# A channel shuffle on one core: the first two tiles cut into pieces of 4, 6, 10 and 20 KB a partition where they were 4, 8 and 28 KB

## The chip, the core and the metric

The kernel runs on one core of a Trainium2 chip. The metric is device time in microseconds (us), from the start of the program to its end; before the change the median of three runs is 316.1 us (316.05 to 316.12). A profile of one execution stands beside it. In the profile the engines are named PE (TensorE), DVE (VectorE), ACT (ScalarE), POOL (GpSimd) and SP (SyncE). This kernel computes on DVE alone; SP and ACT only issue DMAs.

## The reference

The input is a float32 tensor of 16 x 64 x 64 x 256, 67.11 MB. The 256 channels of every pixel are seen as 8 groups of 32, and the two are swapped, so that channel g*32 + j moves to place j*8 + g. No arithmetic is done: every byte is read once and written once, in another order within its row of 1 KB.

```python
x = x.reshape(batch, h, w, groups, channels_per_group)
x = x.transpose(0, 1, 2, 4, 3)
x = x.reshape(batch, h, w, c)
```

## The kernel before

The 65,536 pixels are taken as a flat list of rows of 256 floats (1 KB). A piece of q KB a partition is 128 x q consecutive rows: partition p holds q of them in one run, so a piece is one contiguous block in HBM, and each partition's share of it is contiguous too.

The list `_SLOTS` (line 12) says how the rows are cut. Each entry is a tile, and a tile is a list of pieces whose sizes are in KB a partition. Before the change there are 15 tiles: the first has pieces of 4 and 8 KB, the second one of 28 KB, then come twelve of 38 KB, and one of 16 KB. All tiles have the size of the biggest, 38 KB a partition; a smaller one uses the front of it.

Three things happen to a piece. SP issues its load into `in_tile` (line 55). DVE copies it to `out_tile`, reading in the transposed order and writing in a straight line (lines 57 to 60). ACT issues its store from `out_tile` (line 61). Within a tile all loads are issued first, and then copy and store go piece by piece.

The order on each engine is that of the program; nothing reorders it. What makes one engine wait for another is the data and the buffers. There are two input buffers (`_IN_BUFS`), used in turn: the load of tile k + 2 waits for the copies of tile k. There are three output buffers (`_OUT_BUFS`): the copies of tile k + 3 wait until the stores of tile k have landed. The loads are in one DMA queue (q1 in the profile, issued by SP), the stores in another (q10, issued by ACT); both are served by the same 16 DMA engines.

Of the kernel before, what the change touches and what calls it, by code (L numbers as in the profile page):

```python
# [1 line left out]

# [4 lines left out]


F32 = mybir.dt.float32
P = 128  # L10

_SLOTS = [[4, 8], [28]] + [[38]] * 12 + [[16]]
_IN_BUFS = 2
_OUT_BUFS = 3


@with_exitstack
def kernel(
    ctx: ExitStack,
    tc: tile.TileContext,  # L20
    x: bass.AP,
    groups: bass.AP,
    out: bass.AP,
):
    nc = tc.nc
    b, h, w, c = x.shape
    G = int(groups)
    CPG = c // G
    assert G * CPG == c
    assert sum(map(sum, _SLOTS)) * P == b * h * w  # L30
    biggest = max(map(sum, _SLOTS))

    x_flat = x.rearrange("b h w c -> (b h w c)")
    out_flat = out.rearrange("b h w c -> (b h w c)")

    in_pool = ctx.enter_context(tc.tile_pool(name="in_pool", bufs=_IN_BUFS))
    out_pool = ctx.enter_context(tc.tile_pool(name="out_pool", bufs=_OUT_BUFS))

    def rows(flat, first, q):

        return flat[first * c : (first + P * q) * c].rearrange("(p f) -> p f", p=P)

    ctx.enter_context(tc.manual_schedule(engines=None))
    first = 0
    for parts in _SLOTS:
        in_tile = in_pool.tile([P, biggest * c], F32, name="in_tile")
        out_tile = out_pool.tile([P, biggest * c], F32, name="out_tile")
        at = 0
        pieces = []
        for q in parts:  # L50
            pieces.append((q, first, slice(at * c, (at + q) * c)))
            first += P * q
            at += q
        for q, start, cols in pieces:
            nc.sync.dma_start(out=in_tile[:, cols], in_=rows(x_flat, start, q))  # L55
        for q, start, cols in pieces:
            nc.vector.tensor_copy(  # L57
                out=out_tile[:, cols].rearrange("p (i j g) -> p i j g", j=CPG, g=G),
                in_=in_tile[:, cols].rearrange("p (i g j) -> p i j g", g=G, j=CPG),
            )  # L60
            nc.scalar.dma_start(
                out=rows(out_flat, start, q), in_=out_tile[:, cols]
            )


# [1 line left out]
_INS = ['x', 'groups']  # L67
_OUTS = [((16, 64, 64, 256), 'float32')]

_NUMBERS = {'groups': 8}  # L70


# [26 lines left out]
```

## Time and profile before

| what | value |
| --- | --- |
| median of three runs | 316.1 us (316.05 to 316.12) |
| span of the profiled execution, first to last instruction | 314.4 us |
| bytes read and written | 67.11 MB and 67.11 MB, 427 GB/s over the span |
| DVE busy | 119.0 us, 16 copies |
| copy of 38 KB, mean of 12 | 8.79 us |
| first copy starts | 4.06 us |
| last copy (16 KB) starts, takes | 294.54 us, 3.87 us |
| first store issued (ACT) | 5.19 us |

The page gives no time of the profiled execution other than its span; 1.7 us lie between the span and the median. A span starts with the first instruction and ends with the last. The 40 slices of a row each cover 7.9 us, and a digit 9 means busy for 90% or more. A DMA share is the busy share of the 16 DMA engines, by packets; in a short stretch it can go over 1, because a packet is counted in the stretch in which it starts. The times from issue to landing of the early transfers:

```profile
in_tile<-in_x_dram SPq DMA_DIRECT2D x1, 3584.0 KB, 14.7
out_dram<-out_tile ACTq DMA_DIRECT2D x1, 3584.0 KB, 30.9
in_tile<-in_x_dram SPq DMA_DIRECT2D x1, 1024.0 KB, 5.4
out_dram<-out_tile ACTq DMA_DIRECT2D x1, 1024.0 KB, 25.0
in_tile<-in_x_dram SPq DMA_DIRECT2D x1, 512.0 KB, 3.3
out_dram<-out_tile ACTq DMA_DIRECT2D x1, 512.0 KB, 14.3
```

A landing counts from the issue, so it contains the time in which the transfer stands behind others.

### The profile page before, as it was taken

How to read it: one execution, taken by the hardware profiler on the slowest of the kernel's cores; microseconds unless marked ns; L12 is line 12 of the kernel's file. 1: busy time of each engine (PE TensorE's matmuls, PEld its weight loads, DVE VectorE, ACT ScalarE, POOL GpSimd, SP SyncE). 2: the span in 40 equal slices, each digit the busy share in tenths (PEclk: the TensorE clock that was granted, in tenths of full speed). 3: DMA queues.
4: the chain of work that ended last, by engine and by line, in shares of the span. 5: the costliest groups of instructions: out<-in, count | busy, mean ns of one | idle time of the engine just before them, and what ended most of it. 6: DMA issues, size and time to landing. Idle time of an engine off the chain costs nothing.

```text
span 314.4 us, 132 instructions
## 1 busy us (share of the span) xinstructions
DVE 119.0 (38%) x16; POOL 0.2 (0%) x4
## 2 busy tenths in 40 slices
DVE  2081907309109109019028028037046055065400
POOL 0000000000000000000000000000000000000000
DMA  7999999999999999999999999999999999999997
GB/s 317 405 441 416 435 416 483 401 465 406 450 421 446 426 436 436 401 470 396 475 396 475 396 470 401 470 401 470 401 450 421 446 426 436 436 417 450 429 421 321
DMA packets 4608, 134.22 MB, mean 427 GB/s; under 512 B 512, under 2 KB 512, under 8 KB 768
## 3 DMA queue, kind: packets, MB, share of 16 engines
q1 hardware_dynamic: 2304, 67.11, 49.8%
q10 hardware_dynamic: 2304, 67.11, 49.4%
HBM read 67.11 MB, written 67.11 MB: 427 GB/s over the span
## 4 chain that ended last, share of the span: by engine, by line
DMA 76%; DVE 19%; issue 0%; SPq 0%; DVEq 0%
DMA in_tile<-in_x_dram 76%; DVE out_tile L57 19%; SPq L55 0%; DVEq L57 0%
## 5 line engine op out<-in xcount | busy, mean ns | idle before, releaser
L57 DVE COPY out_tile<-in_tile 128x9728 f32<-128x9728 f32 (+4 forms) x16 | 119.0, 7440 | 179.4 <-DMA in_tile<-in_x_dram 179.4
L80 POOL MEMSET const-uint8-127<- 128x1 uint8 x1 | 0.1, 103 | 0.0
L80 POOL MEMSET const-bfloat16-1.0<- 128x1 bf16 x1 | 0.1, 102 | 0.0
L80 POOL MEMSET const-float32-1.0<- 128x1 f32 x1 | 0.1, 100 | 0.0
L80 POOL MEMSET const-float32-0.0<- 128x1 f32 x1 | 0.1, 99 | 0.2 <-issue 0.2
## 6 DMA issues: line engine op xcount, KB each, us to landing
in_tile<-in_x_dram SPq DMA_DIRECT2D x12, 4864.0 KB, 37.0
out_dram<-out_tile ACTq DMA_DIRECT2D x12, 4864.0 KB, 42.6
in_tile<-in_x_dram SPq DMA_DIRECT2D x1, 3584.0 KB, 14.7
out_dram<-out_tile ACTq DMA_DIRECT2D x1, 3584.0 KB, 30.9
in_tile<-in_x_dram SPq DMA_DIRECT2D x1, 2048.0 KB, 30.4
out_dram<-out_tile ACTq DMA_DIRECT2D x1, 2048.0 KB, 15.2
in_tile<-in_x_dram SPq DMA_DIRECT2D x1, 1024.0 KB, 5.4
out_dram<-out_tile ACTq DMA_DIRECT2D x1, 1024.0 KB, 25.0
```

The costliest lines, as they stand in the source:

```text
L57: nc.vector.tensor_copy(out=out_tile[:, cols].rearrange("p (i j g) -> p i j g", j=CPG, g=G), in_=in_tile[:, cols].rearrange("p (i g j) -> ...
L80: nc = _bacc.Bacc("TRN2", target_bir_lowering=False, num_devices=1)
```

## The change

Only the list of sizes changes. The first tile now has three pieces, of 4, 6 and 10 KB, and the second tile one of 20 KB; together they are 40 KB a partition as before, so every later tile covers the same rows at the same addresses. There are still 15 tiles, which use the buffers in the same turn. There is one piece more, and so one load, one copy and one store more (17 of each where there were 16). The first 38 KB tile uses the input buffer of the first tile, so its load now waits for three copies rather than two; the second 38 KB tile uses the output buffer of the first tile, so its copy now waits for three stores rather than two.

```diff
-_SLOTS = [[4, 8], [28]] + [[38]] * 12 + [[16]]
+_SLOTS = [[4, 6, 10], [20]] + [[38]] * 12 + [[16]]
 _IN_BUFS = 2
 _OUT_BUFS = 3
```

## The prediction

> **What bounds the kernel now.** I read the page first (busy shares, the slices, the two DMA queues), then busy time by stretch, then the timeline of the first 60 us, then single stretches of the DMA queues to price a packet.
>
> ```profile
> span 314.4 us, 132 instructions
> DVE 119.0 (38%) x16; POOL 0.2 (0%) x4
> DMA  7999999999999999999999999999999999999997
> DMA packets 4608, 134.22 MB, mean 427 GB/s; under 512 B 512, under 2 KB 512, under 8 KB 768
> q1 hardware_dynamic: 2304, 67.11, 49.8%
> q10 hardware_dynamic: 2304, 67.11, 49.4%
> DMA in_tile<-in_x_dram 76%; DVE out_tile L57 19%; SPq L55 0%; DVEq L57 0%
> ```
>
> VectorE (DVE) works 38% of the span. q1 carries the loads, q10 the stores; together their packets occupy the 16 DMA engines for 99.2% of the span, 311.9 of 314.4 us. So the chain of waits, which alternates a load and a copy, is not the limit: each of its loads lasts so long because the engines are full. By stretch (busy DVE, POOL, clock, DMA share, GB/s):
>
> ```profile
> 0.00:1.60 1.60, 0.00 (x0) 0.20 (x4) 1.00 0.00 0
> 1.60:312.00 310.40, 119.04 (x16) 0.00 (x0) 1.00 1.00 432
> 312.00:314.40 2.40, 0.00 (x0) 0.00 (x0) 1.00 0.27 116
> ```
>
> Nothing moves before 1.6 us; then the engines are full until 312.0; the last packets and the final wait take the rest. The whole span is 1.6 us of start, the packets' time, and about 1 us at the end. Only three things can move the end: the packets' own time, an interval in which loads and stores are both missing, and the two ends.
>
> What a packet costs, from stretches with one size (queue: packets, MB, share of 16 engines over the stretch). From 60 to 83 us, both queues with 38 KB a partition:
>
> ```profile
> q1 hardware_dynamic: 144, 4.98, 50.1%
> q10 hardware_dynamic: 144, 4.98, 50.1%
> ```
>
> From 308.6 to 312 us, the 16 KB store alone; then from 3.8 to 5.4 us, the 8 KB load alone; then from 1 to 2 and from 2 to 3 us, the 4 KB load alone:
>
> ```profile
> q10 hardware_dynamic: 94, 1.54, 105.6%
> ...
> q1 hardware_dynamic: 82, 0.67, 101.8%
> ...
> q1 hardware_dynamic: 11, 0.05, 36.9%
> ...
> q1 hardware_dynamic: 71, 0.29, 73.4%
> ```
>
> A load or store leaves 144 packets, 9 per engine: 8 of data, one per partition, and a tiny one (32 tiny ones among the 288 in 23 us). 38 KB: 1.002 x 23 x 16 / 256 = 1.440 us each. 16 KB: 1.056 x 3.4 x 16 / 94 = 0.611. The slope is 0.829 us for 22,528 B, 0.0368 us per 1000 B; the constant is 0.611 - 0.603 = 0.008 us. 8 KB: 1.018 x 1.6 x 16 / 82 = 0.318, a constant of 0.016. The queues take turns packet by packet: 144 against 144 above, and 142 against 141 from 8.5 to 19 us, where stores of 4 KB stand against loads of 28 KB.
>
> **The change part by part.** All edits lie in the first two tiles; bytes, the 12 big tiles and the last one stay.
>
> ```profile
> 4.06 1.09 DVE L57 COPY out_tile<-in_tile 128x1024 f32<-128x1024 f32 x1 [4.06 <-DMA in_tile<-in_x_dram]
> 6.61 2.02 DVE L57 COPY out_tile<-in_tile 128x2048 f32<-128x2048 f32 x1 [1.46 <-DMA in_tile<-in_x_dram]
> 16.36 6.57 DVE L57 COPY out_tile<-in_tile 128x7168 f32<-128x7168 f32 x1 [7.73 <-DMA in_tile<-in_x_dram]
> 30.18 8.82 DVE L57 COPY out_tile<-in_tile 128x9728 f32<-128x9728 f32 x1 [7.25 <-DMA in_tile<-in_x_dram]
> 49.11 8.80 DVE L57 COPY out_tile<-in_tile 128x9728 f32<-128x9728 f32 x1 [10.10 <-DMA in_tile<-in_x_dram]
> ```
>
> 1. One more load and one more store of the same bytes. Per engine 2 x 8 data packets at a constant of 0.008, and 2 tiny ones (no more than 0.01 each): 0.15 us. With the constant of the 8 KB row, 0.28. On the path, since the engines are full. Bounds 0.15 and 0.28; I take 0.2.
>
> 2. Copies. 1.09, 2.02 and 6.57 (9.7 us) become 1.09, about 1.56, 2.48 and 4.77 (9.9; between the rows of 1024, 2048, 4096 and 7168 elements: 1.09, 2.02, 3.87, 6.57). Nothing on the path: DVE stands idle 179 us. SP issues one load more (0.33 us) and ACT one store more (0.36); SP's fourth issue ends near 2.1 us, and the third load keeps the engines until about 8.2.
>
> 3. The first 38 KB load waits for all copies of the first tile. Before, it is issued at 8.7 us with the 28 KB load in the queue until 16.4. After: 1.6 + 0.3 (slow first packets, item 5) + 8 x (0.159 + 0.234 + 0.385) = 8.1, plus 0.9 to landing (the 4 KB load's last packet should end at 1.6 + 0.3 + 1.3 = 3.2; its copy starts at 4.06), so the 10 KB copy starts near 9.1 and ends near 11.7. The cover is the 20 KB load: 8 x 0.761 = 6.1 us and the 4 KB store's packets beside it, so until about 15.6. The new load, issued at 11.7, has first packets some 0.9 later (0.73 to 1.6 for the first one). Were it late, the stores in the queue would still fill the engines. Cost 0.
>
> 4. Out buffers. There are three, so the copy of the second 38 KB tile waits for all stores of the first tile: 16 packets per engine before, 24 after. Before, the 8 KB store lands at 8.65 + 25.0 = 33.6 us and that copy starts at 49.1: 15.5 us spare. After, stores begin near 7 to 9 us (none showed between 5 and 8 us before) and take turns with 8 packets of 20 KB and 16 of 38 KB, the loads up to the second big one. So the 10 KB store's last packet goes out with about the last packet of that load: the spare falls to roughly -2 to +6 us and stays so for the tiles after, both queues moving at one packet each. Where it is negative, DVE shows a wait on a store for the first time. Queued behind it: that store, and the load two tiles on, which SP issues after the copy. That copy ends 9 to 12 us after its load landed, while the next load occupies 23 us; and two stores lie queued. Cost 0; gone only if the copy came another 10 us later.
>
> 5. Slow packets early. In 1 to 2 us the first 4 KB packets took 0.369 x 16 / 11 = 0.54 us each rather than 0.16: 0.26 us, and the first load is unchanged. From 8.5 to 34 us loads beside small stores run over their price:
>
> ```profile
> q1 hardware_dynamic: 142, 4.07, 91.2%
> ...
> q1 hardware_dynamic: 147, 5.10, 81.9%
> ...
> q1 hardware_dynamic: 144, 4.98, 57.6%
> ```
>
> (8.5 to 19, 19 to 34, 34 to 54 us.) 153.2 engine-us against 150.7 by the price, 196.6 against 188.9, 184.3 against 184.5. Divided by 16: 0.16, 0.48, 0. So 0.64 us are lost while 16 small store packets per engine go by, and none later. Part of it is one event: from 31.8 to 33 us, 9 load packets take 0.822 x 1.2 x 16 / 9 = 1.75 us each, not 1.44. If the loss follows the count of small stores (24, or 32 with the 20 KB one), it grows by 0.32 to 0.64; if it was an accident of that execution, it can vanish: -0.64. I take 0, since the largest share sits in one short event.
>
> 6. The end. Stores lag the loads by 8 more packets per engine, so more lies behind the last load: before, it landed at 294.4 with stores until 312. The last copy (3.9 us) and the out buffer it waits for lie under two queued 38 KB stores. From 296 to 306 us stores alone fill 1.01 of the engines, as both queues do. Cost 0.
>
> Two sentences apart: DMA: Bandwidth & Descriptors, section Anatomy of one DMA, gives each DMA a fixed cost of about 2 us (for DMAs issued from GpSimd, an engine that issues none here), which for one more load and one more store would make 316.1 + 4 = 320. The section Rules for kernel authors asks for at least 1 MiB per DMA, which the 4, 6 KB pieces (0.5 and 0.75 MiB) miss; the full stretches above show no such cost where transfers stand queued back to back.
>
> Sum: 0.2 + 0 + 0 + 0 + 0 + 0 = 0.2 us. The profiled span is 314.4, and the median 316.1 is 1.7 above it; the 1.7 is taken as unchanged. 316.1 + 0.2 = 316.3.
>
> **The rivals.**
>
> A, slower: the early loss follows the number of small packets. For it: 0.64 us while small stores ran, 0 after. Against it: the event at 32 us. Price 0.28 + 0.64 = 0.9, so 317.0. It decides from +0.63, that is if each of the 16 more store packets up to the 20 KB one costs about 0.03 us (0.64 / 16 = 0.04).
>
> B, faster: the finer start removes the early loss. At most 0.64 + 0.26 go, less the 0.15: 315.4. Against it: the first load, whose packets are the slowest, is untouched, and stores remain small. Nothing else is to be had: of the span only 2.5 us are outside the packets' time.
>
> C, the buffer wait of item 4 reaches the DMA queues: not only must the load queue run dry (10 us of cover), stores must be gone too, with two of 23 us each in the queue. If one such gap of 3 us came, 319. Nothing speaks for it.
>
> D, the change does nothing: 316.1, inside the forecast.
>
> **How the numbers follow.** A measurement of this kernel tells about 0.2% (0.6 us) from no change: 315.5 to 316.7 counts as the same. Forecast and D 0.80; A 0.12 and C 0.02, slower; B 0.06, faster. Range: from 316.3 down by most of the 0.64 that may vanish, 315.7; up to rival A, 317.0. The likeliest case's own range is 316.1 to 316.6.
>
> **What would show it.** DMA queues: 2448 packets each, not 2304, shares that sum to 99% again, 1.00 between 1.6 and 312. Four small copies at about 1.1, 1.6, 2.5, 4.8 us; the first 38 KB load issued near 11.7, before the 20 KB load is out. From the fourth tile on, DVE idle time that ends with a store, or barely not; the last load landing some us earlier and a longer stretch of stores alone, with the end unmoved. Wrong if any stretch after 2 us has a DMA share clearly under 1, or if 38 KB packets take more than 1.44 us for longer than the first 35 us.

## The result and the profile after

The changed kernel takes 326.36 us (326.24 to 326.42, four runs) against 316.11 us before: a ratio of 1.0321, with a 95% interval of 1.0308 to 1.0334. The prediction was 316.3 us, at most 317.0. The profiled execution's span is 324.6 us, 10.2 more than before.

The page of the changed kernel:

```profile
span 324.6 us, 137 instructions
DVE 120.5 (37%) x17; POOL 0.2 (0%) x4
DMA  8999999999999999999999999999999999999997
q10 hardware_dynamic: 2448, 67.11, 51.0%
q1 hardware_dynamic: 2448, 67.11, 48.3%
```

The packets are those foreseen, 2448 a queue, and the DMA engines are again full nearly all the time: 99.3% of a longer span. So nothing stands still; the same bytes cost more DMA time. q1 (loads) occupies 48.3% of 324.6 = 156.8 us, against 49.8% of 314.4 = 156.6 before. q10 (stores) occupies 165.5 us against 155.3. **All of the 10.2 us are in the stores' packets.**

Busy time by stretch (DVE, POOL, clock, DMA share, GB/s) says when; first the changed kernel, then the one before:

```profile
2.00:60.00 58.00, 27.87 (x6) 0.00 (x0) 1.00 1.02 432
60.00:280.00 220.00, 80.21 (x10) 0.00 (x0) 1.00 1.00 413
```

```profile
2.00:60.00 58.00, 27.30 (x5) 0.00 (x0) 1.00 1.01 427
60.00:280.00 220.00, 80.94 (x10) 0.00 (x0) 1.00 1.00 434
```

The first 60 us, in which all the changed pieces are loaded and nearly all of them stored, are no slower (432 GB/s against 427). From 60 to 280 us, in the 38 KB tiles that the change leaves alone, the full engines move 413 GB/s instead of 434. One period of that stretch in the changed kernel, from the copy at 86.6 to the next at 110.9 us, and the part of it in which DVE does nothing, from 95.7 to 110.8 us:

```profile
q10 hardware_dynamic: 144, 4.98, 52.4%
q1 hardware_dynamic: 144, 4.98, 47.4%
...
q10 hardware_dynamic: 96, 3.11, 52.8%
q1 hardware_dynamic: 96, 3.11, 47.7%
```

A load packet takes 0.474 x 24.3 x 16 / 128 = 1.44 us, as before. A store packet takes 0.524 x 24.3 x 16 / 128 = 1.59 us where it took 1.44, and as long while DVE stands idle (0.528 x 15.1 x 16 / 80 = 1.59), so it isn't the copies that disturb it. Nine 38 KB stores run beside 38 KB loads, 72 packets per engine, and 72 x 0.15 = 10.8 us, of which a few packets at the start are spared.

DVE shows the wait that the prediction's item 4 had as possible:

```profile
DVE out_tile L57 <- DMA out_dram<-out_tile: 159.3, 12, 15.5
DVE out_tile L57 <- DMA in_tile<-in_x_dram: 20.1, 5, 8.6
```

Twelve copies are released by a store and not by a load. It is tempting to call this the cause; the experiments say otherwise.

### The profile page after: what moved, and what is told of

Read it like the earlier page. It is cut to its first block, busy times and chain, and to the rows that moved or that the text cites. A ratio compares the mean times of both kernels' runs of the same rounds, so it can differ in the third digit from the quotient of the medians.

```text
span 324.6 us, 137 instructions
## 1 busy us (share of the span) xinstructions
DVE 120.5 (37%) x17; POOL 0.2 (0%) x4
## 3 DMA queue, kind: packets, MB, share of 16 engines
q10 hardware_dynamic: 2448, 67.11, 51.0%
q1 hardware_dynamic: 2448, 67.11, 48.3%
## 4 chain that ended last, share of the span: by engine, by line
another core or an unknown queue 40%; DVE 29%; DMA 23%; SPq 0%; issue 0%; DVEq 0%
DVE out_tile L57 29%; DMA out_dram<-out_tile 15%; DMA in_tile<-in_x_dram 8%; SPq L55 0%; DVEq L57 0%
## 5 line engine op out<-in xcount | busy, mean ns | idle before, releaser
L57 DVE COPY out_tile<-in_tile 128x9728 f32<-128x9728 f32 (+5 forms) x17 | 120.5, 7090 | 179.5 <-DMA out_dram<-out_tile 159.3
## 6 DMA issues: line engine op xcount, KB each, us to landing
out_dram<-out_tile ACTq DMA_DIRECT2D x12, 4864.0 KB, 63.3
```

Of the source, the lines that this page charges most:

```text
L57: nc.vector.tensor_copy(out=out_tile[:, cols].rearrange("p (i j g) -> p i j g", j=CPG, g=G), in_=in_tile[:, cols].rearrange("p (i g j) -> ...
```

## The experiments

A number made them comparable: the **lag**, how many data packets per DMA engine the stores are behind the loads. The kernel issues the load of tile k + 2 and the store of tile k after the same copy, tile k's. If both landed together, the stores would be exactly 2 tiles, 16 packets, behind. Each turn of one load and one store packet by which the store lands later (2.88 us; 3.03 with slow stores) adds one packet. Both issues, kernel before and then changed kernel (last column: us to landing):

```profile
in_tile<-in_x_dram SPq DMA_DIRECT2D x12, 4864.0 KB, 37.0
out_dram<-out_tile ACTq DMA_DIRECT2D x12, 4864.0 KB, 42.6
```

```profile
in_tile<-in_x_dram SPq DMA_DIRECT2D x12, 4864.0 KB, 39.0
out_dram<-out_tile ACTq DMA_DIRECT2D x12, 4864.0 KB, 63.3
```

Before: 16 + 5.6 / 2.88 = 18. After: 16 + 24.3 / 3.03 = 24, three whole tiles. With 8 data packets per tile and engine, a lag of 16 or 24 means that an engine's load packet and the store packet after it belong to the same one of its 8 partitions, if every whole DMA gives an engine the same partitions in the same order (the trace doesn't name a packet's partition). That became the theory; its rivals were the buffer wait, the small pieces themselves, and the HBM addresses of load and store.

The runs in which every big tile is whole and of 38 KB, in one table. The store packet is the mean of the 38 KB data packets between 100 and 250 us, from the queue's share in that stretch (changed kernel: 0.518 x 150 x 16 / 784 = 1.585; 30.51 MB are 784 packets). Each run but the first two rows is one execution; the kernel before, run on the same chip, took 316.06 to 316.43 beside them.

| run | landing of 38 KB load, store | lag | store packet, us | time, us |
| --- | --- | --- | --- | --- |
| before | 37.0, 42.6 | 18 | 1.44 | 316.1 |
| after | 39.0, 63.3 | 24 | 1.59 | 326.4 |
| e1_hold2 | 39.3, 63.6 | 24 | 1.57 | 327.2 |
| e2_before_hold6 | 36.9, 53.9 | 22 | 1.44 | 316.1 |
| e3_14_16 | 39.5, 39.6 | 16 | 1.59 | 328.5 |
| e4_shift76 | 39.2, 63.5 | 24 | 1.59 | 326.9 |
| f1_lag16_shift76 | 39.2, 39.5 | 16 | 1.58 | 328.3 |
| f2_before_shift | 36.9, 42.5 | 18 | 1.44 | 316.1 |
| f4_8_22 | 34.4, 60.1 | 25 | 1.44 | 319.0 |
| g1_before_hold7 | 39.3, 63.6 | 24 | 1.59 | 328.2 |
| g2_12_18 | 37.4, 48.8 | 20 | 1.44 | 322.2 |
| g4_pad640 | 38.9, 63.1 | 24 | 1.58 | 326.2 |
| h7_after_hold3 | 37.0, 57.0 | 23 | 1.44 | 318.8 |

Every run at 16 or 24 has slow stores, and no other has.

### First runs: hold the first store, change the pieces, shift the addresses

e1 is the changed kernel, with dummy copies on ACT ahead of the first store; e2 is the kernel before with six of them.

```diff
+            if first_store:
+                first_store = False
+                for _ in range(_HOLD):
+                    nc.scalar.copy(out=out_tile[:, 28 * c : 32 * c], in_=in_tile[:, 0 : 4 * c])
             nc.scalar.dma_start(
```

> Same tiles as the changed kernel; ACT makes two dummy copies of 1024 elements (into an unused part of the output buffer) before it issues the first store, which therefore leaves about 1.5 us later. Lag theory (38 KB store packets are slow when stores run exactly 3 tiles, 24 packets per engine, behind the loads, so that the two queues are at the same partition): the lag becomes 3 tiles and about 2 packets, store packets return to 1.44 us, time 316.3 to 317. Theory of the buffer wait (DVE's wait on stores is what costs): stores come later still, the wait grows, 326 or more. Theory of the extra small pieces: they are all there, 326.

327.23 us, and the lag did not move: ACT issued the first store at 5.26 us, while its second dummy copy was still running (the two end at 6.2), and the store landed 11.6 us later, as without a hold (11.8). The edit missed its aim, so the run decides nothing.

> The kernel before with its old pieces (4, 8; 28), but six dummy copies on ACT hold the first store back by some 6.5 us, about six load packets of 28 KB. Lag theory: the lag goes from 2 tiles and 2 packets to 3 tiles and about 0, store packets of 38 KB rise to about 1.58 us and the time to about 326; one packet off and it may stay at 316 to 317. Theory of the small pieces: 316 to 317. Theory of the buffer wait: DVE waits for stores, slower, up to 326.

316.08 us. The first store was issued at 9.48 us rather than 5.19, which made a lag of 22, not 24. Fast, as the lag theory has it for 22, but no test yet.

e3 has other pieces in the changed kernel:

```diff
-_SLOTS = [[4, 6, 10], [20]] + [[38]] * 12 + [[16]]
+_SLOTS = [[4, 6, 14], [16]] + [[38]] * 12 + [[16]]
```

> Pieces 4, 6, 14 and 16 KB: as many transfers as in the changed kernel, but the third load is longer, so stores begin while it runs, some 2 to 3 packets before the second tile's load. Lag theory: lag 2 tiles and 5 to 6 packets, no wait of DVE on stores, 38 KB packets at 1.44 us, 316.3. Theory of the small pieces: 326.

328.54 us, a miss of the lag that was expected. Between 15 and 20 us the stores got ahead, 162 packets against 59 (tiny ones included): the copy of the 14 KB piece, for which the first 38 KB load waits, ends only at 14.8 us. The lag settled at 16 rather than 21 or 22, the other multiple of 8. The run's worth lies in its waits, in which no copy is released by a store:

```profile
DVE out_tile L57 <- DMA in_tile<-in_x_dram: 194.5, 17, 15.7
```

Slow without any wait on the output buffers: **the buffer wait is not the cause.** At a lag of two tiles, ten 38 KB stores run beside 38 KB loads, not nine, and 80 x 0.15 = 12 us fits the 12.5 that this run is over the kernel before.

e4 leaves the order alone and moves the HBM addresses of the 38 KB loads.

```diff
-            nc.sync.dma_start(out=in_tile[:, cols], in_=rows(x_flat, start, q))
+            nc.sync.dma_start(out=in_tile[:, cols], in_=rows(x_flat, start + (_SHIFT if q == 38 else 0), q))
```

> The changed kernel, but each 38 KB load reads x from 76 rows further on (two partitions' worth, 77,824 B), so the output is shifted by 76 rows in these tiles. Order, sizes, buffers and partitions stay; only the HBM addresses that are read while a given store packet runs move, to the relation they had in the kernel before (2 packets apart). If the slow store packets come from load and store being at the same SBUF partition: 326 still. If they come from the HBM addresses of load and store: 316.3.

326.85 us: still slow. But load and store were now three tiles and two packets apart in HBM, not two tiles and two packets as before, so the next runs set this relation itself.

### HBM addresses or partitions

f1 is e3 with a shift of +76 rows, f2 the kernel before with -76; the edit is that of e4.

> Pieces 4, 6, 14 and 16 KB (lag of the stores: 16 packets per engine, slow), but the 38 KB loads read x from 76 rows further on, so the output is shifted there. While a store packet runs, load and store addresses in HBM now stand exactly as in the kernel before (two tiles and two packets apart), but both are at the same SBUF partition. Theory of the same partition (lag a multiple of 8 packets): still slow, 328. Theory of the HBM addresses: 316.3.

328.31 us: with the HBM relation of the kernel before, but at a lag of 16, it is as slow as e3. (The shift can't give the same relation at every packet: at an engine's last ones of a tile, a lag of 18 pairs a store with the load of one tile further on. But were the other store packets at 1.44 us, the mean would be well under the 1.58 that was measured.)

> The kernel before (lag 18 packets, fast), with the 38 KB loads reading x from 76 rows earlier, so the output is shifted there. HBM addresses of load and store now stand two whole tiles apart, as in the slow run with pieces of 4, 6, 14, 16 KB; the partitions stay two packets apart. Same partition: 316.1. HBM addresses: 326 to 328.

316.10 us: with the HBM relation of the slow e3, but at a lag of 18, it is as fast as the kernel before. **The HBM addresses of load and store to one another are not the cause.**

f3 was to take load and store to different partitions at the same lag:

```diff
+                nc.sync.dma_start(out=in_tile[64:, cols], in_=src[64:, :])
+                nc.sync.dma_start(out=in_tile[:64, cols], in_=src[:64, :])
```

> The changed kernel, with each 38 KB load issued as two, partitions 64 to 127 first and then 0 to 63; stores are whole. The packets per engine and the lag of 24 should stay, but load and store are no longer at the same partition at the same time. Same partition: store packets at 1.44 us, 316.5 (12 more tiny packets per engine, 0.1 us). A theory in which the lag itself matters (both queues change transfers at the same moment): 326.

386.98 us, for another reason. From 60 to 100 us:

```profile
q1 hardware_dynamic: 220, 6.69, 65.2%
q10 hardware_dynamic: 222, 5.34, 35.3%
```

The 6.69 MB are 172 load packets, so one takes 0.652 x 40 x 16 / 172 = 2.43 us, and 1.96 from 100 to 250 us (54.0% for 25.76 MB, 662 packets): loads of 64 neighbouring partitions, on all 16 engines, cost far more than whole ones. In the Trainium skill, SBUF — State Buffer, the section "Can I just issue two DMAs to hit both halves?", says that only a transfer over all 128 partitions reaches all 16 ports, and this agrees. Splitting a load adds a tiny packet to each tile's loads alone, too, so the lag did not stay: it fell from 22 at 60 us to 17 at 250 us. The run tells nothing of the theory.

### One packet on either side, and the old pieces at a lag of 24

f4 moves the changed kernel's start by one packet.

```diff
-_SLOTS = [[4, 6, 10], [20]] + [[38]] * 12 + [[16]]
+_SLOTS = [[4, 6, 8], [22]] + [[38]] * 12 + [[16]]
```

> Pieces 4, 6, 8 and 22 KB: as many transfers as in the changed kernel, but the 22 KB load starts some 0.6 us earlier, so one packet more of it should be out before the first store packet: lag 25 rather than 24 (if two: 26). Same partition: store packets at 1.44 us, 316.3, although DVE waits for stores even longer. Theory of the small pieces or of the buffer wait: 326 or more. If a lag of 25 is still slow, neighbouring partitions collide as well.

318.97 us at a lag of 25, store packets back at 1.44 us, although as many pieces are loaded and twelve copies still wait for stores, 152.9 us in all (159.3 in the changed kernel). What is left, 2.5 us over the kernel before beside it (316.43), is not in the stores' price. From 314 us to the end the engines' mean share is 0.04 (16 x 3.2 x 0.04 = 2 engine-us), which is one engine finishing alone:

```profile
314.00:317.20 3.20, 0.00 (x0) 0.00 (x0) 1.00 0.04 15
```

g1 does the opposite: the kernel before, its two tiles 4, 8 and 28 KB untouched, with its first store held longer (seven dummy copies that read the output tile, so that loads are not held).

> The kernel before with its old pieces; seven dummy copies on ACT hold its first store until near 11.6 us, so that its first packet goes out near 15.6 us, after the first packet of the first 38 KB load: lag 24 packets rather than 18. Lag theory (slow at multiples of 8): store packets of 38 KB rise to about 1.58 us, 326. Theory that only the small pieces do it: 316. If the lag comes out at 22, 23 or 25 and the time at 316 to 318, that fits the lag theory as well.

328.19 us at a lag of 24: **the old pieces at the new lag are as slow as the new ones.**

> Pieces 4, 6, 12 and 18 KB: as many transfers as in the changed kernel, the 18 KB load starts 0.6 us later. Lag theory: one packet less before the first store, lag 23, store packets at 1.44 us, 316.3 to 317; DVE may still wait for stores. Small pieces: 326. If a lag of 23 is slow, the neighbouring partition collides as well.

322.16 us at a lag of 20, not 23. Store packets are at 1.44 us. Its own loss is elsewhere: between 70 and 140 us load packets take 1.48 us (0.506 x 70 x 16 / 383), and one engine finishes alone from 316.4 us on (mean share 0.04). What slowed those loads and held that engine was not tried.

> The pieces of the changed kernel, but the big tiles are 38 and 36 KB in turn and the last one 28 KB. The lag should stay 24 packets, load and store at the same partition, but their packets are no longer of one size (1.44 beside 1.37 us). Same partition alone: store packets still about 10% over their price, 325. If equal size is needed too (the 20 KB stores beside 38 KB loads ran at their price in the changed kernel): 316.5.

322.77 us. By 150 us the loads have sent 1552 packets and the stores 1120; the difference is 27 per engine, three of them the tiny ones of three tiles, so the lag is 24 as meant. From 100 to 250 us:

```profile
q10 hardware_dynamic: 944, 31.49, 51.8%
q1 hardware_dynamic: 944, 31.52, 48.6%
```

By the price (0.0368 us per 1000 B and 0.008 a packet) the stores' 31.49 MB in 832 data packets are 1165 engine-us; they took 0.518 x 150 x 16 = 1243, 7% more, and the loads 1166. So equal sizes are not needed, but unequal ones lose less than the 10% of the changed kernel.

> The changed kernel with input tiles 640 B longer a partition, so that input and output buffers lie at other offsets to one another within a partition. Lag stays 24. Same partition, whatever the offset: 326. A theory of offsets (banks within the partition): another time, down to 316.3.

326.24 us: input buffers longer by 640 B, which moves them and the output buffers against one another within the partition, change nothing. Other offsets were not tried.

### The partition, or the lag itself?

The last pair leaves the changed kernel as it is but for one load, tile 9 counted from 0, and the store that is its neighbour at a lag of 24, that of tile 6. Both go out in three parts. The two runs differ in nothing but the order of the store's parts:

```diff
+_EVEN_FIRST = (slice(0, None, 2), slice(1, None, 4), slice(3, None, 4))
+_ODD_FIRST = (slice(1, None, 4), slice(3, None, 4), slice(0, None, 2))
...
-            nc.sync.dma_start(out=in_tile[:, cols], in_=rows(x_flat, start, q))
+            for s in _EVEN_FIRST if slot == 9 else _WHOLE:
+                nc.sync.dma_start(out=in_tile[s, cols], in_=src[s, :])
...
+            for s in _ODD_FIRST if slot == 6 else _WHOLE:
+                nc.scalar.dma_start(out=dst[s, :], in_=out_tile[s, cols])
```

> The changed kernel; one load (tile 9) and the store that runs beside it at a lag of 24 packets (tile 6) are each issued in three parts: even partitions, then every fourth from 1, then every fourth from 3. Both go through the partitions in the same order. Same partition, and also the theory that the lag alone counts: the 128 packets of that store stay near 1.58 us, like those of the other tiles; 326.5. If two DMA engines now meet on a port, the load packets of tile 9 go over 1.44 and the pair tells nothing.

> As the run before, but the store of tile 6 takes the odd partitions first and the even ones last, while the load of tile 9 takes the even ones first: same parts, same lag, never the same partition at the same turn. Same partition: the packets of this one store fall to about 1.44 us (the first few may still be slow) while those of the other tiles stay near 1.58; some 1 us less in all, 325.5. Lag alone: no change from the run before.

326.80 and 325.89 us. The store of tile 6 in the run with the same order (159.4 to 183.4 us), and in the run with odd first (158.5 to 182.0 us):

```profile
q10 hardware_dynamic: 176, 4.98, 53.3%
q1 hardware_dynamic: 176, 4.98, 48.1%
```

```profile
q1 hardware_dynamic: 184, 5.14, 51.2%
q10 hardware_dynamic: 180, 4.98, 49.1%
```

Both hold 4.98 MB of stores, 128 data packets. Same order: 0.533 x 24 x 16 / 128 = 1.60 us. Odd first: 0.491 x 23.5 x 16 / 128 = 1.44. In the tile before, both runs are slow (from 135.4 to 159.4 us the store queue's share is 53.1% and 53.0% for 4.98 MB). The store after it is slow again in the run with odd first (from 188.2 to 200.2 us, 64 packets, 2.49 MB, 52.2%: 1.57 us). The load packets beside the store of tile 6 take 1.44 us in the same order and 1.46 with odd first (0.512 x 23.5 x 16 / 132), so these parts, unlike f3's halves, hardly disturb one another. With lag, sizes and DMAs alike, and both queues still changing tiles at the same moment, the order of partitions decides (the HBM addresses move with it, but f1 and f2 leave these out): **what costs is that a DMA engine writes a partition of SBUF for a load and reads the same one for the next store.**

The last run holds the changed kernel's first store, as g1 held that of the kernel before.

> The changed kernel with all its small pieces; three dummy copies on ACT hold the first store some 2 us, two to three 20 KB packets. Lag theory: lag 26 or 27, store packets of 38 KB at 1.44 us, 316.5 to 319 (a lag of 25 gave 319.0), although DVE waits for stores longer than in the changed kernel. Small pieces or buffer wait: 326 or more.

318.84 us. The first stores went out later, then the load queue ran dry (from 60.5 to 62.5 us it moved nothing while the stores moved 1.18 MB), and the lag settled at 23, not the 26 or 27 expected: store packets at 1.44 us with all the small pieces in place. Only two copies wait for a store here, 15.3 us in all, so this run clears the pieces, and of the buffer wait it says nothing; that is left to e3 and f4. Its last 3.8 us, from 313.3, are again one engine alone (share 0.04).

### How the loss sets in

Three stretches of the changed kernel: 46 to 60.7 us (20 KB stores beside 38 KB loads, lag 24), 63 to 68.7 us (the first 38 KB store begins) and 71.7 to 83.7 us:

```profile
q1 hardware_dynamic: 112, 4.36, 68.7%
q10 hardware_dynamic: 96, 1.97, 31.1%
...
q10 hardware_dynamic: 32, 1.25, 50.5%
q1 hardware_dynamic: 32, 1.25, 50.5%
...
q10 hardware_dynamic: 64, 2.49, 53.0%
q1 hardware_dynamic: 64, 2.49, 48.0%
```

A 20 KB store packet takes 0.311 x 14.7 x 16 / 96 = 0.76 us, its price. The first two rounds of 38 KB stores take 0.505 x 5.7 x 16 / 32 = 1.44, and soon after it is 0.530 x 12 x 16 / 64 = 1.59. The store after the fast one in h6 begins in the same way: 32 packets at 0.497 x 5.8 x 16 / 32 = 1.44 us from 182.5 to 188.3 us, then 1.57. This would fit a store's read from SBUF that runs ahead, beside the load's write to the same partition, and is slowed there: hidden as long as it is shorter than the load packet, and seen once the head start of the first rounds is used up. That account is argued from these rows; no run took it apart. The length of the load counts as well: from 280 to 294 us, at the same lag of three tiles, 38 KB stores run beside the 16 KB load, and their packets take 0.694 x 14 x 16 / 108 = 1.44 us, the price.

## Why the prediction was wrong

- **What bounds the kernel** was right: the engines are full in both kernels, and the copies (1.10, 1.55, 2.49, 4.79 us; foreseen 1.09, 1.56, 2.48, 4.77) cost nothing.
- **Item 1** (one load and one store more, 0.2 us) holds as far as it can be read: in f4, with as many transfers and its stores at their price, the queues occupy 49.4% and 49.1% of 317.2 us, 312.4 us against 311.9 before, where the rounding of each share is worth 0.2.
- **Item 3** was right: the first 38 KB load's copies end at 11.84 us (foreseen 11.7), the engines stay full.
- **Item 4** is the step that failed. Its mechanism was right to the packet: "the 10 KB store's last packet goes out with about the last packet of that load", the spare shrinks to about nothing, "both queues moving at one packet each". What was wrong is "Cost 0". It priced only the wait of DVE, which indeed costs nothing (f4 waits nearly as long, 152.9 us against 159.3, at 1.44 us a packet), and took the 38 KB packet's 1.440 us for a constant. That price had been measured at a lag of 18, the only one in that trace. At 24 a store packet costs 1.59, and over nine tiles this is the 10.2 us.
- **Item 5**: its loss from the small stores didn't grow. The changed kernel is as fast as the one before until 60 us, so rival A has its sign right and its mechanism wrong. **Rival C** (a gap in the queues from the buffer wait) did not occur either; the engines have no gap.
- **Item 6** was right in cost, though the stores fell back by 6 packets (18 to 24) and not by 8; from 300 to 310 us stores alone run at the price of before (128 packets, 4.36 MB, share 100.8%).
- The fixed 2 us per DMA that stood beside the sum plays no part: DMA time grew in stores that the change did not touch.
- "Wrong if 38 KB packets take more than 1.44 us for longer than the first 35 us" was the sign that came.

## What to carry to other kernels

When two DMA queues take turns on full engines, the distance between them is a quantity of the kernel. Where every tile is one load and one store it was set here within the first 65 us and then hardly moved (in the changed kernel the loads are 25 data packets per engine ahead at 60 us and at 250 us, just after a load's turn); in f3, where a tile is two loads and one store, it drifted. Count it in packets, from the landings of a load and a store issued together. If it is a whole number of tiles, each engine writes and reads the same partitions in turn, and here stores of 38 KB beside loads of 38 KB then cost 10% more; moving the distance by one or two packets takes that cost away (f4 and h7, one packet off, still end 2.5 and 2.7 us over the kernel before, and there one DMA engine is late). A price per packet taken from one trace holds for the distance of that trace, so a change of the start that looks free must be asked which distance it leads to.

## What was not expected of the hardware

- A load to and a store from the same SBUF partition, one after the other on one DMA engine, slow the store from 1.44 to 1.59 us per 38 KB packet; the load stays at 1.44 (h5 against h6). At distances of 18, 20, 22, 23 and 25 packets, nothing of it is seen.
- It sets in after two packets per engine, and not at every pair of sizes: 20 KB stores beside 38 KB loads (0.76 us) and 38 KB stores beside the 16 KB load (1.44 us) ran at their price.
- Loads of 64 neighbouring partitions, two after one another, took 2.43 us per 38 KB packet from 60 to 100 us and 1.96 from 100 to 250 us (f3); a load in parts of 64 partitions in steps of two and 32 in steps of four took 1.44 and 1.46 (h5, h6).
- ACT issued a DMA that depended on none of its own copies while its last copy was still running (issue at 5.26 us, copies until 6.2), so a copy ahead of a DMA on that engine holds it only in part.
- In f4, g2 and h7, which have the lag right, one DMA engine ended some 2 to 3 us after the others. Its cause stays open, and with it whether the changed pieces could reach 316.3.
